# The last token block's tail moved behind the first feed-forward units, and the second product moved into the first one's buffers

## The chip, the core and the metric

The kernel runs on one core of a Trainium2 chip. The metric is device microseconds of one execution. Five engines work side by side: PE (TensorE, the matrix products), DVE (VectorE), ACT (ScalarE), POOL (GpSimd) and SP (SyncE, which here issues every DMA). Each engine runs its own instructions strictly in order; they meet through semaphores.

## What is computed

One transformer block of 2048 tokens by 1024 features, all in fp32. Cut to what matters here:

```python
y = concat([o, y_lru]) @ w_out                       # attention and recurrence, then the out product
x = layer_norm(ALPHA * x + g1 * y, ln1_g, ln1_b)
h = modulate(layer_norm(x), sh2, sc2)
a, b = split(h @ w_ffn_in, 2)                        # first product, 1024 x 5632
f = (silu(a) * b) @ w_ffn_out                        # second product, 2816 x 1024
out = layer_norm(ALPHA * x + g2 * f, ln2_g, ln2_b)
```

## The kernel before, in words

Every fp32 operand of PE is kept as two rounded tiles, a high part (a cast on ACT) and the remainder (a subtraction on DVE or POOL); `mm3` (lines 140 to 144) makes one product out of three matrix instructions, L142, L143 and L144. Everything around the change is written in Python order; a scheduler moves instructions within an engine where priorities and buffers let it, and buffers come from rings ("pools") whose size sets how far ahead a producer may run.

**Out product, L1037 to L1076.** Sixteen token tiles (`out_tile`), four to a token block. The residual `x` of a tile is loaded just ahead of it into a ring of SBUF tiles.

**Tail of a token block, L1078 to L1118.** When four tiles are done, a generator `after` gives the block's tail in 21 steps: `norm1` (L1083: layer norm, times `lg` at L1086, plus `lb` at L1089, both 128x1024 on POOL), `norm2` (a second layer norm), and `lift2` (L1101: eight steps, each four PE transposes at L1105, an ACT evacuation L1107 and a store into `h2_d`). The tail of block b is stepped inside the out tiles of block b+1. Block 3 has no block behind it, so its tail is drained by `while tails: step()` before the feed-forward's code begins.

**First product.** The two halves of the tokens (`tb`) are taken one after the other; each is multiplied by 22 column groups, 44 units in all. A unit (`Unit`, L1170 to L1248) is a 2x2 block product with seven sub-products (Strassen and Winograd's form), each of 12 matrix instructions, 84 to a unit. `prep` loads and combines weights on POOL (L1189 to L1194), casts them (L1198, ACT) and subtracts (L1199, DVE); a ring of 9 weight tiles `w` lets it run ahead. `build(tb, k)` (L1145 to L1169) makes the token operands of one quarter k of the contraction: reload from `h2_d`, combine, and split into the `B` and `T` tiles. Units 0 and 1 begin the first half: four products that need only the operands `B11` and `B21`, made ahead by `lift2`, with the four builds between them. `sliced` runs a unit quarter by quarter, and unit 21 is sliced with the builds of the second half behind its quarters. The last instruction of a unit on DVE is L1246, and its results go to `hid_d` in DRAM.

**Second product, L1290 to L1379.** All first-product buffers are closed, and new ones opened. 32 tiles (16 token tiles by two column halves) of 22 contraction steps, 66 matrix instructions each. `prep_w2` (L1307) loads a weight tile into one of 4 raw buffers, casts it (L1311) and subtracts (L1312); 25 `w2` tiles are held. `load_hid` (L1317) loads a token tile's hidden values as two pieces of 704 KB, one tile ahead. The output chain of a tile begins with L1359; the last one's is the end of the kernel.

These lines set the order around the change:

```python
        while tails:              # L1128: block 3's tail, drained here
            step()
...
    ahead(4)
    for k, (u, p) in enumerate(((units[0], 1), (units[0], 2), (units[1], 1), (units[1], 2))):
        build(0, k)
        whole(u, (p,))
```

Of the kernel before, what the change touches and what calls it, by code (L numbers as in the profile page):

```python
# [60 lines left out]
def kernel(ctx: ExitStack, tc: tile.TileContext, x, cx, prm_d, wa1, wa2, b_ada, w_in, w_v, lqk,  # L61
# [924 lines left out]
    s5 = ExitStack()  # L986
    fe = s5.enter_context(tc.tile_pool(name="fe", bufs=1, reuse_waits="tile"))
    toks = {(n, k): fe.tile([P, 2, 512], F32R, tag=f"{n}{k}", name=f"{n}_{k}") for n in ("B11", "B21") for k in range(4)}
    rawp = s5.enter_context(tc.tile_pool(name="rawp", bufs=3, reuse_waits="tile"))
    sp_ = s5.enter_context(tc.tile_pool(name="sp5", bufs=1, reuse_waits="tile"))  # L990
    qp = s5.enter_context(tc.tile_pool(name="qp5", bufs=6, reuse_waits="tile"))

    with ExitStack() as s4:
        wps = {k: s4.enter_context(tc.tile_pool(name=f"wo{k}", bufs=1, side="right", reuse_waits="tile"))
               for k in (4, 5, 6, 7, 0, 1, 2, 3)}
        oyp = s4.enter_context(tc.tile_pool(name="oyp", bufs=2, side="right", reuse_waits="tile"))
        psW = s4.enter_context(tc.tile_pool(name="psW", bufs=2, space=PSUM, side="right", reuse_waits="tile"))
        psL = s4.enter_context(tc.tile_pool(name="psL", bufs=1, space=PSUM, reuse_waits="tile"))
        psX = s4.enter_context(tc.tile_pool(name="psX", bufs=2, space=PSUM, reuse_waits="tile"))

        xq = s4.enter_context(tc.tile_pool(name="xq", bufs=7, side="right", reuse_waits="tile"))
# [4 lines left out]
        lnq = s4.enter_context(tc.tile_pool(name="ln4", bufs=1, side="right", reuse_waits="tile"))  # L1006
        lg = lnq.tile([P, D], F32, tag="lg", name="lg")
        lb = lnq.tile([P, D], F32, tag="lb", name="lb")
        tp = s4.enter_context(tc.tile_pool(name="tp", bufs=2, side="right", reuse_waits="tile"))
        xtile = lambda n: (tp.tile([P, D], F32, tag="x", name="x4", bufs=4) if 1 <= n % 11 <= 4 else  # L1010
                           xq.tile([P, D], F32, tag="xq", name="xq"))
# [18 lines left out]
        tails = []  # L1030

        def step():
            for t in list(tails):
                if next(t, 0) == 0:
                    tails.remove(t)

        def out_tile(b, i, rh, xs, mv):  # L1037
            ti = 4 * b + i
            oy = oyp.tile([P, 2, 8, P], F32R, tag="oy", name="oy")
            dma(oy.rearrange("p a k t -> p (a k) t"),  # L1040
                oy_d[b].rearrange("p a k t -> p (a k) t")[:, :, i * P:(i + 1) * P])
            xt = xtile(ti)
            dma(xt, x[ti * P:(ti + 1) * P, :])
            xv = xt.rearrange("p (a b) -> p a b", a=2)

            def mms(ps, kk, st, en):
                lh, ll = oy[:, 0, kk], oy[:, 1, kk]
# [24 lines left out]
            with tc.high_priority(offset=100):  # L1072
                V.tensor_tensor(xv, pl, xv, ALU.add)
            ln_stats(xt, mv, i)
            xs.append(xt)

        def affine(xs, mv, rs):
            nb = sm.tile([P, 4], F32, tag="nb", name="nb")  # L1078
            V.scalar_tensor_tensor(nb, mv[:, 0], -1.0, rs, ALU.mult, ALU.mult)
            for i, xt in enumerate(xs):  # L1080
                S.activation(xt, xt, AF.Identity, bias=nb[:, i:i + 1], scale=rs[:, i:i + 1])

        def norm1(xs, mv):  # L1083
            affine(xs, mv, rsqrt(mv[:, 1], 4, LN_EPS))
            for i, xt in enumerate(xs):
                G.tensor_tensor(xt, xt, lg, ALU.mult)  # L1086
            yield
            for i, xt in enumerate(xs):
                G.tensor_tensor(xt, xt, lb, ALU.add)  # L1089
                yield  # L1090

        def norm2(b, xs):
            mw = sm.tile([P, 2, 4], F32, tag="mv", name="mw", bufs=4)
            for i, xt in enumerate(xs):
                dma(x1_d[4 * b + i], xt)
                ln_stats(xt, mw, i)
                yield
            affine(xs, mw, rsqrt(mw[:, 1], 4, LN_EPS))
            yield

        def lift2(b, xs):  # L1101
            for k in range(KD):
                ps = psX.tile([P, 512], F32, tag="x", name="ps_x")
                for i in range(4):
                    PE.transpose(ps[:, i * P:(i + 1) * P], xs[i][:, k * P:(k + 1) * P], ident)  # L1105
                hf = tp.tile([P, 512], F32, tag="hf", name="hf4", bufs=2)
                S.activation(hf, ps, AF.Identity, bias=mod2[:, k:k + 1], scale=mod2[:, 8 + k:9 + k])  # L1107
                dma(h2_d[b][:, k], hf)
                if b == 0:
                    t = toks["B11" if k < 4 else "B21", k % 4]  # L1110
                    S.copy(t[:, 0], hf)
                    G.tensor_tensor(t[:, 1], hf, t[:, 0].bitcast(F32), ALU.subtract)
                yield

        def after(b, xs, mv):
            yield from norm1(xs, mv)
            yield from norm2(b, xs)
            yield from lift2(b, xs)  # L1118

        for b in range(NB):  # L1120
            rh = head_norm(b)
            xs = []
            mv = sm.tile([P, 2, 4], F32, tag="mv", name="mv4", bufs=4)
            for i in range(4):
                out_tile(b, i, rh, xs, mv)
            tails.append(after(b, xs, mv))
            step()
        while tails:  # L1128
            step()

    opp = [s5.enter_context(tc.tile_pool(name=f"opp{k}", bufs=1, side="right", reuse_waits="tile")) for k in range(4)]
# [128 lines left out]
    def whole(u, ps):  # L1263
        for p in ps:
            u.mms(p, range(4), True, True)
            ahead(1)
# [17 lines left out]
    for u in units[2:NJ - 1]:  # L1284
        whole(u, std)
# [154 lines left out]
```

## Time and profile before

| | |
|---|---|
| median of 3 runs | 2962.98 us (2962.23 to 2969.71) |
| the profiled execution | 2965.58 us, its span 2963.8 us, mean granted clock 0.97 |
| busy: PE, DVE, POOL, ACT | 94%, 66%, 48%, 47% of the span |
| chain that ended last | PE 67%, DVE 7%, ACT 3%, DMA 3% |
| stages, us from the start | attention to about 1360, out product to 1540, first product to 2448, second to 2952, output of the last tile to 2963.8 |

The span is the time on the core from the first instruction to the last; the execution's own time is 1.8 us more. With PE at 94% a stage is read by what PE waited for in it, in the list of waits, and by whether it did its instructions at the full clock.

### The profile page before, as it was taken

What the parts mean: (1) busy time and instruction counts of PE and PEld (TensorE: products, weight loads), DVE (VectorE), ACT (ScalarE), POOL (GpSimd) and SP (SyncE); (2) the same over time, 40 slices, a digit from 0 to 9 for tenths busy, and PEclk for the clock granted to TensorE, in tenths of its full rate; (3) what the DMA queues carried; (4) which work ended last, traced back from release to release, by engine and by line L of the source; (5) the groups of instructions that cost most, each with busy time, mean ns of one, the idle gap of its engine ahead of it and who ended that gap; (6) DMA issues with size and microseconds to landing.
All of it is one profiled execution on the core that took longest, in us unless ns stands there. A gap on an engine that the chain in (4) does not pass through costs nothing.

```text
span 2963.8 us, 37341 instructions
## 1 busy us (share of the span) xinstructions
PE 2776.1 (94%) x13452; PEld 2316.7 (78%) x13452; DVE 1955.0 (66%) x3202; ACT 1407.1 (47%) x1907; POOL 1421.9 (48%) x891
## 2 busy tenths in 40 slices
PE   8989889878999999999985999999999998999998
PEld 4868767766899999887864888887888886887886
DVE  7755796487899989986886655558655545225554
ACT  3537568744777777763344333334333324113332
POOL 2014643455788888861535444445444433222443
PEclk9999999989999999999997999999999999999999
DMA  8874636366132312135563222223222218434542
GB/s 332 313 217 167 215 116 256 113 219 184 36 85 64 81 58 70 54 140 195 193 200 114 93 86 82 84 84 104 93 82 82 84 52 291 146 129 162 172 165 93
DMA packets 223193, 407.94 MB, mean 138 GB/s; under 512 B 20888, under 2 KB 110104, under 8 KB 220448
## 3 DMA queue, kind: packets, MB, share of 16 engines
q1 hardware_dynamic: 223008, 405.55, 41.2%
q8 instruction: 106, 1.74, 0.2%
q14 instruction: 79, 0.65, 0.1%
HBM read 281.74 MB, written 123.75 MB: 137 GB/s over the span
## 4 chain that ended last, share of the span: by engine, by line
PE 67%; DVE 7%; ACT 3%; DMA 3%; issue 1%; POOL 1%; SPq 0%; ACTq 0%; DVEq 0%; POOLq 0%
PE ps L143 9%; PE ps L144 9%; PE ps L142 9%; PE ps_s L846 8%; PE ps_f L142 5%; PE ps_f L143 5%; PE ps_f L144 5%; PE pt L927 4%; PE po L921 2%; PE po L922 2%; PE po L920 2%; DMA w2r<-in_w 1%; DVE e L848 1%; PE ps_w L1050 1%; PE ps_l L1050 1%
## 5 line engine op out<-in xcount | busy, mean ns | idle before, releaser
L848 DVE TENSOR_SCALAR_CACHE_REDUCE e<-ps_s 128x768 f32<-128x768 f32 x384 | 359.6, 951 | 37.7 <-PE ps_s L846 29.6
L864 POOL TENSOR_TENSOR a<-e,e 128x768 f32<-128x768 f32 x192 | 349.2, 1848 | 17.2 <-PE pt L927 12.5
L846 PE MATMUL ps_s<-k,q 128*128 128x384 f32 x1536 | 336.7, 351 | 15.1 <-DVE e L848 13.7
L853 ACT ACTIVATE e<-e,nm 128x2304 f32<-128x2304 f32 x128 | 285.3, 2229 | 51.8 <-DVE nm L852 48.7
L846 PEld LDWEIGHTS ps_s<-k,q 128*128 128x128 f32 x1536 | 267.9, 191 | 31.0 <-DVE e L848 23.9
L1324 POOL TENSOR_TENSOR hid<-hf,hid 128x1408 fp32r<-128x1408 f32 x32 | 104.8, 3276 | 293.9 <-ACT hid L1323 293.9
L931 ACT CAST ah<-pt 128x512 fp32r<-128x512 f32 x288 | 165.8, 582 | 127.7 <-PE pt L927 125.4
L932 DVE TENSOR_TENSOR al<-pt,ah 128x512 fp32r<-128x512 f32 x288 | 195.7, 685 | 33.7 <-ACT ah L931 33.4
L1323 ACT CAST hid<-hf 128x1408 fp32r<-128x1408 f32 x64 | 87.8, 1375 | 248.0 <-PE ps_f L144 232.0
L861 POOL TENSOR_SCALAR e<-e,rr,rn 128x2304 f32<-128x2304 f32 x64 | 146.4, 2287 | 92.5 <-DVE nm L852 49.6
L142 PE MATMUL ps_p<-ht,w 128*128 128x512 f32 (+1 forms) x416 | 162.8, 392 | 16.0 <-DVE kf L204 10.8
L927 PEld LDWEIGHTS pt<-ident,a 128*128 128x128 f32 x1152 | 144.5, 141 | 42.0 <-POOL a L864 3.3
L927 PE MATMUL pt<-ident,a 128*128 128x128 f32 x1152 | 174.7, 274 | 2.6 <-POOL a L864 2.4
L1189 POOL TENSOR_TENSOR s<-w1r 128x512 f32<-128x512 f32 x44 | 58.0, 1317 | 233.5 <-DMA w1r<-in_w 228.2
L144 PE MATMUL ps_p<-ht,w 128*128 128x512 f32 (+1 forms) x416 | 161.8, 390 | 8.2 <-DVE w L174 8.2
L143 PE MATMUL ps_p<-ht,w 128*128 128x512 f32 (+1 forms) x416 | 161.5, 388 | 0.0
L210 POOL TENSOR_TENSOR lo<-kf,hi 128x512 fp32r<-128x512 f32 (+1 forms) x36 | 58.7, 1632 | 176.5 <-ACT hi L209 140.8
L1194 POOL TENSOR_TENSOR s<-w1r,s 128x512 f32<-128x512 f32 x44 | 73.1, 1661 | 126.9 <-DVE w__15147 L1199 5.6
L920 PE MATMUL po<-ah,v 128*128 128x512 f32 x288 | 126.3, 438 | 0.6 <-ACT ah L931 0.6
L921 PE MATMUL po<-al,v 128*128 128x512 f32 x288 | 116.9, 406 | 3.1 <-DVE al L932 1.4
L922 PE MATMUL po<-ah,v 128*128 128x512 f32 x288 | 114.5, 398 | 0.0
L1324 DVE TENSOR_TENSOR hid<-hf,hid 128x1408 fp32r<-128x1408 f32 x32 | 54.4, 1701 | 86.2 <-ACT hid L1323 86.2
(3085 smaller groups left out, 8258.8 us busy)
## 6 DMA issues: line engine op xcount, KB each, us to landing
w1r<-in_w SPq DMA_DIRECT2D x88, 512.0 KB, 3.5
hf<-hid_d SPq DMA_DIRECT2D x64, 704.0 KB, 4.2
hid_d<-hid SPq DMA_DIRECT2D x88, 256.0 KB, 2.2
wraw<-in_w_in SPq DMA_DIRECT2D x32, 512.0 KB, 5.1
adaw<-in_wa SPq DMA_DIRECT2D x32, 512.0 KB, 4.7
q<-q_d SPq DMA_DIRECT2D x64, 256.0 KB, 4.9
oy<-oy_d SPq DMA_DIRECT2D x16, 1024.0 KB, 6.2
x<-in_x SPq DMA_DIRECT2D x24, 512.0 KB, 8.9
```

The source lines that it names most:

```text
L142: PE.matmul(ps, lhsT=lh, rhs=rh, start=start, stop=False)
L143: PE.matmul(ps, lhsT=lh, rhs=rl, start=False, stop=False)
L144: last["pe"] = PE.matmul(ps, lhsT=ll, rhs=rh, start=False, stop=stop).ins
L846: PE.matmul(ps[:, j, :384], lhsT=q[:, m, part, qt * P:(qt + 1) * P], rhs=kst[h, m][:, c0:c0 + 384], start=(part == 0), stop=(part == 1))
L848: V.tensor_scalar(et[:, cc * 768:(cc + 1) * 768].rearrange("p (a b) -> p a b", a=2), ps[:, :, :384], -0.125, None, ALU.mult, ALU.min, accu ...
L853: S.activation(et, et, AF.Exp, bias=nm[:, m:m + 1], scale=-1.0, accum_out=ss[m])
L864: last["a"] = G.tensor_tensor(a, es[0][:, g * 768:(g + 1) * 768], es[1][:, g * 768:(g + 1) * 768], ALU.add).ins
L920: PE.matmul(po, lhsT=vh, rhs=ah, start=(j == 0), stop=False)
L921: PE.matmul(po, lhsT=vh, rhs=al, start=False, stop=False)
L922: PE.matmul(po, lhsT=vl, rhs=ah, start=False, stop=(j == NKT - 1))
L927: PE.transpose(pt[:, qt * P:(qt + 1) * P], ath[h, b, qt, j // 6][:, (j % 6) * P:(j % 6 + 1) * P], ident)
L932: V.tensor_tensor(al, pt, ah.bitcast(F32), ALU.subtract)
```

## The change

**The tail of block 3 is no longer drained.** It is put on the list `tails` after the out product and stepped (`late`) behind each product of unit 1's last five and of units 2 to 5, held behind the last instructions that those products issued on ACT, DVE and POOL. `norm1` gives its four `lg` products one to a step for this block.

**The first product is prepared earlier.** Its helpers and left-hand pools are made before the out product; the first three weight tiles are prepared after out tile (3,1), and the first build's loads are issued after (3,2). The residual tiles of the out product lie in other pools, some of them shared with the first product's weights; on SP the load of out tile 1's residual now follows those of `lg`, `lb`, three later residuals and one weight. The ring of weight tiles has 5 tiles while the tail lives, then 11, and 7 near the end. Of PSUM banks the products use 6 while the tail lives, then 8.

**The second product takes the first one's slots.** Its pools are gone; w2 tiles lie in the slots of the token operands, and the last unit is sliced so that each quarter, when done, frees slots, and issues loads of hidden values and five w2 tiles (`begin`). A token tile's hidden values come in three loads (512, 512 and 384 KB) and six casts. Token tiles 0 and 1 are multiplied together, so a w2 tile serves two products.

```diff
@@ norm1
-        def norm1(xs, mv):
+        def norm1(xs, mv, dealt):
             affine(xs, mv, rsqrt(mv[:, 1], 4, LN_EPS))
             for i, xt in enumerate(xs):
+                if dealt and i:
+                    yield
                 G.tensor_tensor(xt, xt, lg, ALU.mult)
@@ the out product's loop and the first product
                 out_tile(b, i, rh, xs, mv)
-            tails.append(after(b, xs, mv))
-            step()
+                if (b, i) == (3, 1):
+                    ahead(3)
+                if (b, i) == (3, 2):
+                    qs0 = load_q4(0, 0)
+            if b < NB - 1:
+                tails.append(after(b, xs, mv))
+                step()
         while tails:
             step()
+        tails.append(after(NB - 1, xs, mv))
...
+    def late():
+        with tc.issue_after(last["A5"]), tc.issue_after(last["V5"]), tc.issue_after(last["G5"]):
+            step()
...
+    def new_w():
+        n = 5 if tails else 11 if turn5["n"] < 14 * NJ - 14 else 7
...
-    ahead(4)
+    ahead(1)
     for k, (u, p) in enumerate(((units[0], 1), (units[0], 2), (units[1], 1), (units[1], 2))):
-        build(0, k)
+        build(0, k, None if k else qs0)
         whole(u, (p,))
-    ahead(3)
+    ahead(1)
     sliced(units[0], rest, range(4))
-    whole(units[1], rest)
-    for u in units[2:NJ - 1]:
+    whole(units[1], rest, late)
+    for u in units[2:6]:
+        whole(u, std, late)
+    ahead(2)
+    for u in units[6:NJ - 1]:
         whole(u, std)
@@ the second product
-    sliced(units[-1], std, range(3, -1, -1))
-    s5.close()
-    ps5.close()
+    def load_hid(n, q):
+        i = n % 16
+        w = min(8, NJ - q * 8)
+        raw = x4p.tile([P, 8, P], F32, tag="x", name="hf6")[:, :w]
+        dma(raw, hid_d[i // 4][i % 4, :, q * 8:q * 8 + w, :])
+        for r in range(2):
...
+            S.copy(t[:, 0], raw[:, 4 * r:4 * r + w])
+            (G if m in (1, 4) else V).tensor_tensor(t[:, 1], raw[:, 4 * r:4 * r + w], t[:, 0].bitcast(F32),
+                                                    ALU.subtract)
+    def begin(k):
+        if k < 3:
+            load_hid(0, k)
+        else:
+            load_hid(1, 0)
+        for j in range(5 * k, 5 * k + 5):
+            prep_w2(0, j)
+    sliced(units[-1], std, range(4), begin)
...
+        if n != 1:
+            pss = {m: new_bank() for m in ((0, 1) if n == 0 else (n,))}
+            for j in range(NJ):
+                for m, ps in pss.items():
+                    h, w = hts[m, j // 4], w2t[hf, j]
+                    mm3(ps, h[:, 0, j % 4], h[:, 1, j % 4], w[:, 0], w[:, 1], j == 0, j == NJ - 1)
```

Three places show how instructions stand. On PE at the end of the out product, before (`ps_l` is the last out tile's bank, `ps_x` a transposed tile, `w__15084` the first product's first weight tile):

```order
L1051 MATMUL ps_l<-wo_13335,oy 128x512
L1054 MATMUL ps_l<-wo_13335,oy 128x512 x2
L1105 MATMUL ps_x<-ident,xq 128x128 x24
L142 MATMUL ps<-B_0_13273,w__15084 128x512
L143 MATMUL ps<-B_0_13273,w__15084 128x512
```

and with the change (L1282 is the transpose, `w__14706` the first weight tile):

```order
L1229 MATMUL ps_l<-wo_13347,oy 128x512 x2
L1282 MATMUL ps_x<-ident,x_14129 128x128
L1282 MATMUL ps_x<-ident,x_14200 128x128
L1282 MATMUL ps_x<-ident,x_14288 128x128
L1282 MATMUL ps_x<-ident,x_14395 128x128
L1282 MATMUL ps_x<-ident,x_14129 128x128
L1282 MATMUL ps_x<-ident,x_14200 128x128
L1282 MATMUL ps_x<-ident,x_14288 128x128
L1282 MATMUL ps_x<-ident,x_14395 128x128
L142 MATMUL ps<-B_0_13276,w__14706 128x512
L143 MATMUL ps<-B_0_13276,w__14706 128x512
L144 MATMUL ps<-B_0_13276,w__14706 128x512
```

Of block 2's 24 transposes eight now stand ahead of the first product, eight inside its second sub-product and eight behind its third; block 3's 32 begin some 330 rows further on.

On POOL the eight `lg` and `lb` operations of block 3, before, among the builds (L1161, L1166):

```order
L1166 TENSOR_TENSOR qT<-qT,qB_15156 128x512
L1086 TENSOR_TENSOR x_14539<-x_14539,lg 128x1024
L1161 TENSOR_TENSOR qB_15199<-qB_15201,qB_15199 128x512
L1086 TENSOR_TENSOR x_14610<-x_14610,lg 128x1024
L1086 TENSOR_TENSOR x_14698<-x_14698,lg 128x1024
L1089 TENSOR_TENSOR x_14539<-x_14539,lb 128x1024
L1086 TENSOR_TENSOR x_14805<-x_14805,lg 128x1024
L1089 TENSOR_TENSOR x_14610<-x_14610,lb 128x1024
L1089 TENSOR_TENSOR x_14698<-x_14698,lb 128x1024
L1166 TENSOR_TENSOR qT<-qT,qB_15203 128x512
L1089 TENSOR_TENSOR x_14805<-x_14805,lb 128x1024
```

and with the change, where L1263 and L1266 are the two operations, L1053 to L1058 weights, L1097 and L1098 a unit's sums:

```order
L1056 TENSOR_TENSOR s_15330<-w1r 128x512
L1098 TENSOR_TENSOR q<-u,q 128x512
L1263 TENSOR_TENSOR x_14545<-x_14545,lg 128x1024
L1263 TENSOR_TENSOR x_14616<-x_14616,lg 128x1024
L1263 TENSOR_TENSOR x_14721<-x_14721,lg 128x1024
L1266 TENSOR_TENSOR x_14545<-x_14545,lb 128x1024
L1263 TENSOR_TENSOR x_14836<-x_14836,lg 128x1024
L1053 TENSOR_TENSOR s_15480<-w1r 128x512
L1266 TENSOR_TENSOR x_14616<-x_14616,lb 128x1024
L1266 TENSOR_TENSOR x_14721<-x_14721,lb 128x1024
L1266 TENSOR_TENSOR x_14836<-x_14836,lb 128x1024
L1054 TENSOR_TENSOR s_15481<-s_15480,w1r 128x512
```

The eight still stand nearly together, now between the POOL work of units 2 and 3, with one weight operation among them.

On SP at the end of the first product, before (`hf` a hidden piece, `w2r` a raw w2 tile, `hid_d` a unit's store):

```order
L70 DMA hid_d_90<-hid 128x4x128
L70 DMA hf_21663<-hid_d_88 128x1408
L70 DMA hf_21668<-hid_d_88 128x1408
L70 DMA hf_21783<-hid_d_88 128x1408
L70 DMA g2b<-mod_d 128x1024
L70 DMA w2r<-in_w 128x512 x4
```

and with the change:

```order
L70 DMA hf_21540<-hid_d_88 128x1024
L70 DMA hf_21594<-hid_d_88 128x1024
L70 DMA hid_d_91<-hid 128x4x128
L70 DMA hf_21648<-hid_d_88 128x768
L70 DMA hid_d_90<-hid 128x4x128
L70 DMA hf_21723<-hid_d_88 128x1024
L70 DMA w1r<-in_w 128x1024
L70 DMA hid_d_91<-hid 128x4x128
L70 DMA hid_d_90<-hid 128x4x128
L70 DMA w2r<-in_w 128x512 x2
```

The first hidden pieces now stand ahead of the last unit's weights, and the first w2 tiles ahead of its last stores.

## Rows read from the trace of the kernel before

**Rows 1.** Waits of PE, 1440 to 2964 us: waiter, releaser, us, times, longest.
```profile
PE ps L142 <- ACT w__15084 L1198: 33.0, 1, 33.0
PE ps_x L1105 <- ACT hf L1107: 10.0, 7, 3.0
PE ps_f L142 <- ACT w__21675 L1311: 8.7, 1, 8.7
...
PE ps_f L142 <- ACT w__23152 L1311: 1.7, 1, 1.7
```

**Rows 2.** Timeline of DVE (start, us, instruction): ends of units 4, 20, 26 and 43.
```profile
1698.36 0.68 DVE L1246 TENSOR_TENSOR hid<-g,u 128x512 f32<-128x512 f32 x1
...
2003.00 0.68 DVE L1246 TENSOR_TENSOR hid<-g,u 128x512 f32<-128x512 f32 x1
...
2126.37 0.68 DVE L1246 TENSOR_TENSOR hid<-g,u 128x512 f32<-128x512 f32 x1
...
2452.17 0.68 DVE L1246 TENSOR_TENSOR hid<-g,u 128x512 f32<-128x512 f32 x1
```

**Rows 3.** Timeline of PE: last out tile, transposes, unit 20's and the first product's end.
```profile
1539.92 0.62 PE L1054 MATMUL ps_l<-wo,oy 128*128 128x512 f32 x2
1540.38 1.03 PE L1105 MATMUL ps_x<-ident,xq 128*128 128x128 f32 x8
...
2001.26 0.39 PE L144 MATMUL ps<-T,w__18080 128*128 128x512 f32 x1
...
2448.31 0.39 PE L144 MATMUL ps<-T,w__21505 128*128 128x512 f32 x1
```

**Rows 4.** Timeline of DVE, second product: output chains of tiles 2, 14, 17 and 31.
```profile
2511.22 0.69 DVE L1359 TENSOR_TENSOR f<-ps_f,g2b 128x512 f32<-128x512 f32 x1 [1.61 <-PE ps_f L144]
...
2690.74 0.69 DVE L1359 TENSOR_TENSOR f<-ps_f,g2b 128x512 f32<-128x512 f32 x1 [4.45 <-PE ps_f L144]
...
2743.23 0.69 DVE L1359 TENSOR_TENSOR f<-ps_f,g2b 128x512 f32<-128x512 f32 x1 [1.46 <-PE ps_f L144]
...
2952.66 0.69 DVE L1359 TENSOR_TENSOR f<-ps_f,g2b 128x512 f32<-128x512 f32 x1 [5.61 <-PE ps_f L144]
```

**Rows 5.** Timelines of POOL, DVE and ACT in PE's 33 us of idle time.
```profile
1558.09 5.08 POOL L1086 TENSOR_TENSOR x<-x,lg 128x1024 f32<-128x1024 f32 x2
...
1568.63 5.53 POOL L1089 TENSOR_TENSOR x<-x,lb 128x1024 f32<-128x1024 f32 x2
...
1560.90 5.57 DVE L1156 TENSOR_TENSOR T<-qT,T 128x512 fp32r<-128x512 f32 x2
...
1574.64 0.68 DVE L1156 TENSOR_TENSOR B<-qB,B 128x512 fp32r<-128x512 f32 x1
...
1571.99 0.62 ACT L1155 CAST T<-qT 128x512 fp32r<-128x512 f32 x1 [12.06 <-DVE qT L1163]
...
1580.44 0.61 ACT L1198 CAST w__15084<-w1r 128x512 fp32r<-128x512 f32 x1
```

**Rows 6.** Windows: us, then busy us and count of PE, PEld, DVE, ACT, POOL; clock, DMA share, GB/s.
```profile
1600.00:1610.00 10.00, 5.22 (x21) 4.03 (x22) 2.38 (x4) 4.78 (x8) 5.21 (x4) 0.50 0.58 192
...
1620.00:2020.00 400.00, 400.00 (x1766) 331.23 (x1765) 219.58 (x307) 142.75 (x240) 181.29 (x126) 1.00 0.27 87
...
2460.00:2470.00 10.00, 7.61 (x25) 5.41 (x25) 2.18 (x5) 2.86 (x4) 3.17 (x1) 0.82 1.05 411
...
2500.00:2700.00 200.00, 200.00 (x884) 165.62 (x883) 61.05 (x66) 41.16 (x34) 46.03 (x14) 1.00 0.45 148
```

**Rows 7.** Timelines of SP and ACT at the second product's start.
```profile
2444.65 2.85 SPq L70 DMA_DIRECT2D hf<-hid_d  x3
...
2453.74 2.00 SPq L70 DMA_DIRECT2D hid_d<-hid  x2
...
2459.81 2.52 SPq L70 DMA_DIRECT2D w2r<-in_w  x4
...
2456.75 0.62 ACT L1311 CAST w__21675<-w2r 128x512 fp32r<-128x512 f32 x1 [1.68 <-DMA w2r<-in_w]
```

**Rows 8.** Timeline of ACT: the residual of out tile 1 lands.
```profile
1360.24 1.06 ACT L1068 ACTIVATE x<-x 128x1024 f32<-128x1024 f32 x1 [2.75 <-DMA x<-in_x]
```

More of the change, by code (lines that the diff above doesn't have):

```diff
@@ L986 @@
     s5 = ExitStack()
[L987 to L991, printed above, removed]
+    ps5 = ExitStack()
+    pool5 = lambda n, bufs, **kw: s5.enter_context(tc.tile_pool(name=n, bufs=bufs, reuse_waits="tile", **kw))
@@ new lines, with load_q4 @@
+    x4p = pool5("x4", 4)
+    fe = pool5("fe", 1)
+    toks = {(n, k): fe.tile([P, 2, 512], F32R, tag=f"{n}{k}", name=f"{n}_{k}") for k in range(4) for n in ("B11", "B21")}
+    rawp = pool5("rawp", 3)
+    sp_ = pool5("sp5", 1)
+    lnq = pool5("ln4", 1)
+    xqa = pool5("xqa", 3)
+    qp = pool5("qp5", 6)
+    psX = ps5.enter_context(tc.tile_pool(name="psX", bufs=2, space=PSUM, reuse_waits="tile"))
+    opp, wopB = [], []
+    def load_q4(tb, k):
+        q = {}
+        for n, (s, kk) in (("B11", (0, k)), ("B12", (1, k)), ("B22", (1, k + 4)), ("B21", (0, k + 4))):
+            q[n] = qp.tile([P, 512], F32, tag="q", name="q" + n)
+            dma(q[n], h2_d[2 * tb + s][:, kk])
+        return q
@@ new lines, in build, with split @@
+    def build(tb, k, q=None):
+        q = q or load_q4(tb, k)
+        t1 = qp.tile([P, 512], F32, tag="q", name="qT")
+        def split(n, src):
+            if tb == 0 and n in ("B11", "B21"):
+                return
+            t = (fe if n in ("B11", "B21") else opp[k]).tile([P, 2, 512], F32R, tag=f"{n}{k}", name=f"{n}_{k}")
+            S.copy(t[:, 0], src)
+            V.tensor_tensor(t[:, 1], src, t[:, 0].bitcast(F32), ALU.subtract)
+            toks[n, k] = t
+        split("B11", q["B11"])
+        V.tensor_tensor(t1, q["B12"], q["B11"], ALU.subtract)
+        G.tensor_tensor(q["B12"], q["B22"], q["B12"], ALU.subtract)
+        split("T1", t1)
+        V.tensor_tensor(t1, q["B22"], t1, ALU.subtract)
+        split("T2", t1)
+        split("B21", q["B21"])
+        G.tensor_tensor(t1, t1, q["B21"], ALU.subtract)
+        split("T3", q["B12"])
+        split("B22", q["B22"])
+        split("T4", t1)
@@ new lines, with new_bank @@
+    turn5 = {"w": 0, "p": 0, "n": 0}
+    def new_w():
+        n = 5 if tails else 11 if turn5["n"] < 14 * NJ - 14 else 7
+        i = turn5["w"] % n
+        turn5["w"] = i + 1
+        turn5["n"] += 1
+        pool, tag = ((xqa, "xq") if i < 3 else (wopB[0], "w") if i < 5 else (lnq, "lg" if i == 5 else "lb") if i < 7
+                     else (x4p, "x"))
+        return pool.tile([P, 2, 4, P], F32R, tag=tag, name="w1_")
+    def new_bank():
+        n = 6 if tails else 8
+        i = turn5["p"] % n
+        turn5["p"] = i + 1
+        pool, tag = (psR, "p") if i < 4 else (psQ, "p") if i < 6 else (psX, "x")
+        return pool.tile([P, 512], F32, tag=tag, name="ps")
@@ new lines, with step @@
+    tails = [None]
+    def step():
+        for t in list(tails):
+            if t and next(t, 0) == 0:
+                tails.remove(t)
+    def late():
+        with tc.issue_after(last["A5"]), tc.issue_after(last["V5"]), tc.issue_after(last["G5"]):
+            step()
+    std = (1, 6, 5, 2, 7, 3, 4)
+    rest = (6, 5, 7, 3, 4)
+    units = [Unit(tb, j) for tb in range(2) for j in range(NJ)]
+    preps = [(units[0], 1), (units[0], 2), (units[1], 1), (units[1], 2)]
+    preps += [(u, p) for u in units[:2] for p in rest] + [(u, p) for u in units[2:] for p in std]
@@ new lines, with ahead, whole, sliced @@
+    preps = iter(preps)
+    def ahead(n):
+        for _ in range(n):
+            u, p = next(preps, (None, 0))
+            if u:
+                u.prep(p)
+    def whole(u, ps, each=lambda: None):
+        for p in ps:
+            u.mms(p, range(4), True, True)
+            ahead(1)
+            each()
+    def sliced(u, ps, ks, after=lambda k: None):
+        for n, k in enumerate(ks):
+            for p in ps:
+                u.mms(p, [k], n == 0, n == 3)
+                if n == 3:
+                    ahead(1)
+            after(k)
@@ L1028, in head_norm @@
             return rh
[L1030 to L1035, printed above, removed]
+        tails.clear()
         def out_tile(b, i, rh, xs, mv):
@@ L1249 @@
-    banks = [0]
-    std = (1, 6, 5, 2, 7, 3, 4)
-    rest = (6, 5, 7, 3, 4)
-    units = [Unit(tb, j) for tb in range(2) for j in range(NJ)]
-    preps = [(units[0], 1), (units[0], 2), (units[1], 1), (units[1], 2)]
-    preps += [(u, p) for u in units[:2] for p in rest] + [(u, p) for u in units[2:] for p in std]
-    preps = iter(preps)
-    def ahead(n):
-        for _ in range(n):
-            u, p = next(preps, (None, 0))
-            if u:
-                u.prep(p)
[L1263 to L1266, printed above, removed]
@@ L1268, in sliced @@
-    def sliced(u, ps, ks, after=lambda k: None):
-        for n, k in enumerate(ks):
-            for p in ps:
-                u.mms(p, [k], n == 0, n == 3)
-                if n == 3:
-                    ahead(1)
-            after(k)
-    ahead(4)
+        tails.append(after(NB - 1, xs, mv))
+    opp.extend(pool5(f"opp{k}", 1, side="right") for k in range(4))
+    wopB.append(pool5("wopB", 2, side="right"))
+    ua = pool5("ua5", 2)
+    s5b = ExitStack()
+    ub = s5b.enter_context(tc.tile_pool(name="ub5", bufs=1, reuse_waits="tile"))
@@ L1289, with prep_w2 @@
         whole(u, std)
-    sliced(units[-1], std, range(3, -1, -1))
+    w2t, hts = {}, {}
+    w2slots = [(opp[k], f"{n}{k}") for k in range(4) for n in ("T2", "T1", "T3", "B22", "T4")]
+    w2slots += [(wopB[0], "w")] * 2 + [(xqa, "xq")] * 3
+    hslots = [(fe, f"{n}{k}") for k in range(4) for n in ("B11", "B21")] + [(rawp, "w1r")] * 3 + [(lnq, "lg")]
+    def prep_w2(hf, j):
+        n = hf * NJ + j
+        raw = ua.tile([P, 512], F32, tag="ug"[n % 2], name="w2r")
+        dma(raw, w2[j * P:(j + 1) * P, hf * 512:(hf + 1) * 512])
+        pool, tag = w2slots[n % 25]
+        w = w2t[hf, j] = pool.tile([P, 2, 512], F32R, tag=tag, name="w2_")
+        S.copy(w[:, 0], raw)
+        V.tensor_tensor(w[:, 1], raw, w[:, 0].bitcast(F32), ALU.subtract)
@@ new lines, in begin @@
+    def begin(k):
+        if k < 3:
+            load_hid(0, k)
+        else:
+            load_hid(1, 0)
+        for j in range(5 * k, 5 * k + 5):
+            prep_w2(0, j)
+    sliced(units[-1], std, range(4), begin)
+    s5b.close()
+    lnp = s5.enter_context(tc.tile_pool(name="ln6", bufs=1, reuse_waits="tile"))
+    for j in range(20, NJ):
+        prep_w2(0, j)
+    for q in (1, 2):
+        load_hid(1, q)
+    g2b = lnp.tile([P, D], F32, tag="g2b", name="g2b")
+    stt = lnp.tile([P, 16, 2, 6], F32, tag="stt", name="stt")
```

320 lines of the change are left out of this document (133 added, 187 removed).

## The prediction

> **What bounds the kernel now.** I read the page for the busy shares first: PE works 94% of the span, so the question is only where the other time lies. The list of PE's waits over the last two stages [rows 1] answers it: one wait of 33.0 us before the very first weight tile of the first product, 10.0 us in small waits of the transposes, 8.7 us at the start of the second product, and small ones at its middle. Between these places PE is full: the windows [rows 6] show 1766 matrix instructions in 400 us and 884 in 200 us at clock 1.00, 0.2265 us each. Waits alone understate a stall, because the clock falls after one: in 1600 to 1610 PE did 21 instructions in 10 us at a granted clock of 0.50, the lower of its two levels, 1.2 GHz, after having idled in the transposes before.
>
> So I count each stall by distance instead, against what PE does undisturbed. Units 4 to 20 end 2003.00 - 1698.36 = 304.64 us apart, 19.04 us a unit [rows 2]; tiles 2 to 14 end 179.52 us apart, 14.96 us a tile [rows 4]. Both make 0.2267 us an instruction. A unit's last instruction on DVE starts 1.74 us after its last product starts (2003.00 and 2001.26, [rows 2, 3]).
>
> - Start of the first product. The next instruction after the last out tile could go at 1540.15, unit 4 was done at about 1698.36 - 1.51 = 1696.85. Five units are 95.2 us, and 56 transposes at 1.03 us for eight are 7.2 us; call it 8 with their slower part. Lost: 156.7 - 95.2 - 8 = 53.5 us.
> - Second half's builds. Units 20 to 26 took 123.37 us for 114.24: lost 9.1 us.
> - Start of the second product. The last product of the first ended at about 2448.54 [rows 3]; to tile 2's chain at 2511.22 [rows 4] are 62.5 us, for three tiles' 44.9: lost 17.6 us.
> - Its second weight half. Tiles 15 to 17 took 2743.23 - 2690.74 = 52.5 us for 44.9: lost 7.6 us. Tiles 18 to 31 lose nothing (209.43 us for 14).
>
> **Why the first wait is so long.** The weight needs nothing but a cast. But ACT stands for 12.06 us ahead of it in the cast of a build, waiting for a DVE subtraction, and reaches the weight only at 1580.44 [rows 5]. DVE is late because its subtractions take 2.8 us each (5.57 for two) where one takes 0.68 us elsewhere; and they do so just while POOL runs the tail's 128x1024 operations, at 2.54 and 2.77 us each. So the drained tail costs in two ways: its own length, and through DVE.
>
> **The change part by part.**
>
> *Start of the first product.* The tail's POOL block no longer stands among the first builds, the first three weights are cast before the out product ends, and the first build's loads are there. The 33.0 us wait and the transposes' 10 us go: the transposes stand among products that fill the gaps. What is late next is the builds. The four have 7 two-operand DVE instructions each, 28 in all, and some 12 weight subtractions and evacuations stand between them: 40 x 0.69 = 28 us without disturbance. PE has 48 instructions that need no build, and 60 of unit 0's rest, 24.5 us, and 24 transposes, 3.6 us: 28 us. Bounds: no loss, or, with the builds' own eight POOL operations stretching DVE as above for some 13 us, 13 x (1 - 0.69/2.8) = 10 us. The nearest row is the second half's builds, where 36 such instructions cost 9.1 us; 28 make 7. I take 7.
>
> *The tail beside units 1 to 5.* Its PE and ACT work costs what is counted above. Its POOL block is 4 x 2.54 + 4 x 2.77 = 21.2 us, nearly in one piece between the POOL work of units 2 and 3; POOL is busy 181.29 of 400 us and DVE 219.58 in undisturbed units [rows 6]. In 21.2 us DVE has 7.8 products' work to do and, at 2.8 us for a subtraction and about as much again for the rest, gets through some five, so it falls some 7 us behind. The weights in the ring of five are 13.6 us of work for PE. Bounds: the ring covers it, 0, or nothing covers it, and the weights' sums wait behind the block on POOL too, 11. I take 4, nearer the cover.
>
> A rule of the Trainium skill speaks against this placement: its GPSIMD Engine Reference, section Specifications, says that GpSimd shares its SBUF interfaces with VectorE, in contention with DVE instructions that have two SBUF inputs. The trace agrees: 2.8 us beside POOL, 0.68 without [rows 5]. By the rule alone, every subtraction in the block would wait, and the sum would stand at the upper bound, 7 us more than I take.
>
> *Out product.* The residual of tile 1 landed just in time, ACT having waited 2.75 us for it [rows 8]. It now stands behind six more loads on SP. At the 411 GB/s of [rows 6] 512 KB take 1.3 us, so it comes up to 8 us later, and PE has work of the attention's end beside it: 0 to 5, I take 3.
>
> *Second half's builds.* Unchanged but for a ring of 11 weights instead of 9: 9.1 stays.
>
> *Start of the second product.* Before, SP issued three hidden loads at 2444.65 ahead of any w2 load, the first w2 cast came at 2456.75, and the next four w2 loads went only at 2459.81, behind two stores [rows 7]; the DMA engines were full in 2460 to 2470, 411 GB/s [rows 6]. Now the first hidden pieces and w2 loads stand ahead of the last unit's stores, weights are cast while that unit runs, and a w2 tile serves two products, so 22 tiles are wanted over 29.9 us instead of 15. The 17.6 us should go to 0 to 8; I take 2.
>
> *Second weight half.* Nothing about its four raw buffers changes: 7.6 stays. Six smaller pieces a tile instead of two cost ACT under 1 us a tile beside 14.96 us of products: covered by the double buffering that also stands before. I allow 3 us for the stage.
>
> *Sum.* First product: 53.5 - 7 - 4 - 3 = 39.5 us gained. Second: 17.6 - 2 - 3 = 12.6. Together 52.1. The profiled execution's 2965.58 becomes 2913.5; it stands 2.6 us above the median shown, so I expect **2911 us**.
>
> **The rivals.**
>
> *The tail's block costs as much beside the products as before them.* For it: DVE's 2.8 us, the rule above, and that PE falls to half clock after a stall [rows 6]. Against: DVE is half idle in these units, and five weights are ahead. Its place is units 2 to 4; it gives the upper bounds, 10 + 11 + 5 us, and some 8 more of half clock: 20 us more than the forecast, 2931.
>
> *The start of the second product stays stalled.* For: the same four raw buffers, the same DMA volume at 411 GB/s, and the last unit's quarters now issue loads while its stores wait. Against: the new order on SP. It takes back 17.6 - 2 = 16 us: 2927.
>
> *Nothing is late.* The ring covers the tail, the builds end in time and the second product starts smoothly: 2911 - 7 - 4 - 3 - 5 = 2892.
>
> *Slower.* The hidden pieces become a wait in every tile of the second product: three loads pass through four slots, and a slot is held until two casts and two subtractions, one of them on POOL, are done. Thirty tiles give back the gain at 52.1 / 30 = 1.7 us a tile, and more than 2.0 us a tile is slower by over 0.3%. For: SP carries half as many loads again. Against: before, the tiles had the same depth of two, and 884 instructions in 200 us show no wait. The time then is 2972 us and up.
>
> **How the numbers follow.** Forecast, 2898 to 2924: 0.53. Tail's block: 0.19. Second start: 0.13. Nothing late: 0.10. Slower: 0.05. The range reaches from a little below "nothing late", 2888, to the two middle rivals partly together (2911 + 20 + 10): 2942; about 0.1 lies above and below. The runs of this kernel tell 0.3%, 8.9 us, from no change; a time within that of 2963 needs both middle rivals and more. So faster 0.92, same 0.03, slower 0.05.
>
> **What would show it.** Right: no wait of 33 us at the first product's first weight; unit 4's end about 39 us earlier; DVE's subtractions at over 2 us only beside the tail's POOL block; PE's waits in units 0 to 5 of 10 to 15 us in all, on `T` tiles and weights; tile 2 of the second product some 55 us earlier; tile 16's dip still there. Wrong: a wait of over 15 us on a weight in units 2 to 5, a first w2 wait of over 5 us, or tiles of the second product that end more than 14.96 us apart in its steady part.

## The result

The changed kernel takes 2916.34 us (median of 4 runs, 2915.73 to 2919.35) against 2962.61 us for the kernel before in the same comparison: a ratio of 0.984, 95% interval 0.982 to 0.986. It is faster by 46 us, and lies 5 us above the 2911 us forecast. Its profiled execution has a span of 2913.9 us, 49.9 us less.

The time is made up by stages from five marks on the trace: the last value product of attention on PE, the end of the last out tile, the end of unit 10, the output chain of tile 2 of the second product, and that of tile 31. Units after the tenth, and tiles between the marks, take the same time in both kernels except where the text says so.

| us between marks | before | changed | difference | forecast |
|---|---|---|---|---|
| out product | 181.2 | 189.2 | +8.0 | +3 |
| transposes and units 0 to 10 | 272.1 | 241.9 | -30.2 | -42.5 |
| unit 10 to tile 2 of the second product | 698.6 | 679.0 | -19.6 | -15.6 |
| tile 2 to tile 31 | 441.4 | 433.8 | -7.6 | +3 |

So the sum came out nearly right because its errors cancel: by these marks the first half of the change gained 17 us less than forecast, the second half 15 us more. The mark at unit 10 is DVE's last instruction there, and it stands 1.74 us behind the start of the unit's last matrix instruction before, and 3.41 us in the changed kernel and in all its variants below (unit 20 shows the same: 1977.00 and 1980.41 us in the timelines below, 2001.26 and 2003.00 in [rows 2, 3]). By PE's own work 1.7 us of the third row's gain therefore belong to the second: -31.9 and -17.9 us, so that the first half gained 16 us less and the second 13 us more. That they cancel is luck.

The page of the changed kernel gives PE 95% of its span. The list of PE's waits, from the out product to the end, answers to [rows 1] (waiter, releaser, us in all, times, longest):

```profile
PE ps_w L1225 <- DVE x L1245: 10.4, 5, 3.8
PE ps L144 <- DVE w__15535 L1063: 3.4, 1, 3.4
PE ps L142 <- ACT w__14984 L1062: 2.7, 1, 2.7
PE ps_x L1282 <- ACT hf L1287: 2.6, 1, 2.6
...
PE ps L142 <- ACT T L1019: 2.2, 2, 1.6
...
PE ps L144 <- DVE w__15398 L1063: 1.2, 1, 1.2
```

The 33.0 us are gone, and no wait of the second product is left at all. Instead the out product has 10.4 us (before: 5.3 us in the same lines), and the first units have small waits on weights. The timelines of DVE and PE answer to [rows 2], [rows 3] and [rows 4]: the ends of units 4, 20 (on both engines) and 26, and the chains of tiles 2, 14, 17 and 31.

```profile
1675.77 0.68 DVE L1108 TENSOR_TENSOR hid<-g,u 128x512 f32<-128x512 f32 x1
...
1977.00 0.39 PE L144 MATMUL ps<-T,w__18084 128*128 128x512 f32 x1
1980.41 0.68 DVE L1108 TENSOR_TENSOR hid<-g,u 128x512 f32<-128x512 f32 x1
...
2103.39 0.68 DVE L1108 TENSOR_TENSOR hid<-g,u 128x512 f32<-128x512 f32 x1
...
2468.97 0.69 DVE L1431 TENSOR_TENSOR f<-ps,g2b 128x512 f32<-128x512 f32 x1 [2.73 <-PE ps L144]
...
2648.49 0.69 DVE L1431 TENSOR_TENSOR f<-ps,g2b 128x512 f32<-128x512 f32 x1 [2.73 <-PE ps L144]
...
2693.37 0.69 DVE L1431 TENSOR_TENSOR f<-ps,g2b 128x512 f32<-128x512 f32 x1 [2.13 <-PE ps L144]
...
2902.81 0.69 DVE L1431 TENSOR_TENSOR f<-ps,g2b 128x512 f32<-128x512 f32 x1 [5.60 <-PE ps L144]
```

Unit 4 ends 22.6 us earlier than before, where the prediction named about 39, and tile 2's chain 42.2 us earlier, where it named 55. Units 20 to 26 take 122.98 us, so the second half's builds cost 8.7 us, as before (9.1). Tiles 14 to 17 take 44.88 us, three times 14.96: the dip at the second weight half, 7.6 us before, is gone too, which the prediction did not expect.

**Where the out product lost.** DVE's and PE's timelines at the second out tile of block 3:

```profile
1515.25 1.70 DVE L1063 TENSOR_TENSOR w__14706<-w1r,w__14706 128x512 fp32r<-128x512 f32 x1
...
1518.07 1.70 DVE L1063 TENSOR_TENSOR w__14709<-w1r,w__14709 128x512 fp32r<-128x512 f32 x1
...
1519.81 1.63 DVE L1063 TENSOR_TENSOR w__14716<-w1r,w__14716 128x512 fp32r<-128x512 f32 x1
...
1523.88 0.80 PE L1225 MATMUL ps_w<-wo,oy 128*128 128x512 f32 x1 [3.84 <-DVE x L1245]
```

The three weights that the change prepares early have their subtractions here, each 1.6 to 1.7 us instead of 0.68, since POOL is at block 2's last `lb` operations and, beside the third, at an operation of a build. The out tiles' own DVE work (L1245), which frees PE's banks, stands behind them. The windows show what that does, in the first line; the second is the place in the tail's block, and the third the start of the second product:

```profile
1520.00:1530.00 10.00, 6.16 (x17) 4.79 (x17) 10.00 (x15) 1.09 (x2) 0.90 (x1) 0.66 0.78 280
...
1620.00:1630.00 10.00, 6.42 (x24) 4.49 (x23) 9.17 (x15) 2.29 (x4) 10.00 (x6) 0.92 0.50 195
...
2430.00:2440.00 10.00, 10.00 (x46) 8.27 (x45) 7.28 (x9) 3.43 (x7) 3.55 (x3) 1.00 0.74 235
```

In 1520 to 1530 us PE did 17 matrix instructions where 44 fit: a wait of 3.84 us costs 6, the rest through a mean granted clock of 0.66.

**The tail's block** on POOL, and DVE beside it:

```profile
1606.45 7.97 POOL L1263 TENSOR_TENSOR x<-x,lg 128x1024 f32<-128x1024 f32 x3 [3.83 <-ACT x L1256]
...
1612.10 2.87 DVE L1063 TENSOR_TENSOR w__15418<-s,w__15418 128x512 fp32r<-128x512 f32 x1
1614.89 0.68 DVE L1091 TENSOR_TENSOR v<-ps,u 128x512 f32<-128x512 f32 x1
...
1617.20 2.84 POOL L1263 TENSOR_TENSOR x<-x,lg 128x1024 f32<-128x1024 f32 x1
...
1617.71 2.88 DVE L1063 TENSOR_TENSOR w__15460<-w1r,w__15460 128x512 fp32r<-128x512 f32 x1
```

The subtractions take 2.9 us again, as before in [rows 5]; an instruction with one operand in PSUM, between them, takes its 0.68. The last two lines show the size of such a hold: POOL's instruction ends at 1620.04 us and DVE's at 1620.59. It is so throughout the traces of the kernel before and of the changed one: of the 128x512 DVE `TENSOR_TENSOR` instructions behind 1540 us whose two operands both lie in SBUF, 331 begin while a POOL instruction runs, and 330 of these end 0.54 to 0.64 us after that instruction does (the other one began within 0.01 us of it); the 802 others take 0.70 us at most.

### The profile page after: what moved, and what is told of

The parts are those of the page before. It is cut to its first block, busy times and chain, and to the rows that moved or that the text cites. A ratio compares the mean times of both kernels' runs of the same rounds, so it can differ in the third digit from the quotient of the medians.

```text
span 2913.9 us, 37631 instructions
## 1 busy us (share of the span) xinstructions
PE 2765.6 (95%) x13452; PEld 2310.3 (79%) x13452; DVE 2013.6 (69%) x3298; ACT 1433.6 (49%) x2039; POOL 1409.1 (48%) x923
## 3 DMA queue, kind: packets, MB, share of 16 engines
q8 instruction: 106, 1.74, 0.3%
## 4 chain that ended last, share of the span: by engine, by line
PE 66%; DVE 7%; ACT 3%; issue 2%; POOL 2%; DMA 2%; SPq 0%; DVEq 0%; ACTq 0%; POOLq 0%
PE ps L143 14%; PE ps L144 14%; PE ps L142 14%; PE ps_s L846 8%; PE pt L927 4%; PE po L921 2%; PE po L922 2%; PE po L920 2%; DVE e L848 1%; PE ps_w L1225 1%; PE ps_w L1226 1%; PE ps_w L1229 1%; PE ps_l L1225 1%; PE ps_l L1229 1%; PE ps_l L1226 1%
## 5 line engine op out<-in xcount | busy, mean ns | idle before, releaser
L1376 ACT CAST hid<-hf 128x512 fp32r<-128x512 f32 x192 | 111.5, 586 | 281.2 <-PE ps L144 266.5
L1377 POOL TENSOR_TENSOR hid<-hf,hid 128x512 fp32r<-128x512 f32 x64 | 83.6, 1306 | 315.9 <-ACT hid L1376 315.9
L1377 DVE TENSOR_TENSOR hid<-hf,hid 128x512 fp32r<-128x512 f32 (+1 forms) x128 | 95.8, 751 | 157.1 <-ACT hid L1376 157.0
L861 POOL TENSOR_SCALAR e<-e,rr,rn 128x2304 f32<-128x2304 f32 x64 | 146.4, 2288 | 90.3 <-DVE nm L852 49.9
L1053 POOL TENSOR_TENSOR s<-w1r 128x512 f32<-128x512 f32 x44 | 59.3, 1348 | 270.3 <-DMA w1r<-in_w 254.2
L1097 POOL TENSOR_TENSOR v<-v,q 128x512 f32<-128x512 f32 x44 | 72.1, 1639 | 145.1 <-DVE u L1096 145.1
```

Of the source, the lines that this page charges most:

```text
L1377: (G if m in (1, 4) else V).tensor_tensor(t[:, 1], raw[:, 4 * r:4 * r + w], t[:, 0].bitcast(F32), ALU.subtract)
```

## The experiments

All are read by the same five marks. The runs that share a stage's code tell how far it scatters: the changed kernel twice, and the two edits of the second product, give 189.2, 190.7, 189.8 and 189.7 us for the out product and 241.9, 241.9, 240.5 and 240.4 us for units 0 to 10. Each kernel has one trace, so a mark is one execution's.

| kernel | median us | out product | units 0 to 10 | to tile 2 | tiles 2 to 31 |
|---|---|---|---|---|---|
| changed, again | 2914.89 | 190.7 | 241.9 | 679.1 | 434.3 |
| weights' subtractions later | 2912.13 | 185.2 | 240.5 | 677.8 | 433.8 |
| tail drained | 2943.20 | 186.8 | 268.6 | 679.1 | 434.0 |
| tiles 0 and 1 apart | 2919.30 | 189.8 | 240.5 | 683.5 | 433.8 |
| loads late | 2923.65 | 189.7 | 240.4 | 687.6 | 431.9 |
| tail spread | 2913.13 | 190.8 | 238.9 | 679.0 | 434.7 |
| tail on DVE | 2913.56 | 189.3 | 236.5 | 679.0 | 433.9 |
| later, spread | 2909.66 | 185.2 | 239.0 | 678.5 | 433.8 |
| later, on DVE | 2905.62 | 185.0 | 235.8 | 677.6 | 433.8 |
| later, spread, on DVE | 2905.91 | 183.6 | 233.4 | 678.6 | 433.8 |

**The changed kernel again**, on the chip of the last edits.

> The changed kernel itself, on the chip of this batch, so that the small edits are compared on one chip: 0.984 of the kernel before, 2915 to 2920 us. If the ratio is 0.982 instead, the edits measured so far gained less than their ratios say.

2914.89 us (2912.80 to 2920.55), 0.983 of the kernel before (0.981 to 0.984): between the two values named. Differences of 2 us between medians are therefore not read below; the marks are.

**The tail's place.**

```diff
+    while tails:
+        step()
     ahead(1)
     for k, (u, p) in enumerate(((units[0], 1), (units[0], 2), (units[1], 1), (units[1], 2))):
```

> The changed kernel with block 3's tail drained before the feed-forward again; early weights, first loads and the new second product are kept. Theory A, the tail's place is what the first product gained: PE waits 20 to 30 us before or in the first units again, unit 20 ends 20 to 25 us later than 1980 us, the time is 2936 to 2943 us. Theory B, the early weights and loads are what gained, since the 33 us wait was the first weight's cast in ACT's queue: at most 10 us are lost, 2916 to 2926 us.

2943.20 us, 0.993 of before (0.991 to 0.994), 28 us over the changed kernel, and nearly all of it in units 0 to 10: 268.6 us, against 272.1 before and 241 with the tail moved. PE's waits there:

```profile
PE ps_x L1282 <- ACT x L1256: 18.2, 4, 16.9
PE ps L142 <- ACT T L1019: 8.7, 2, 7.9
```

Theory A holds, at the upper edge of its times. With the tail drained, PE stands for its transposes, which come behind the eight POOL operations, and then for the builds. With no tail left on the list this kernel also has the ring of 11 weight tiles and 8 banks from the first unit on; what these do there was not tried apart. The early weights and loads by themselves are worth some 5 us there (272.1 - 268.6, and 1.7 for the later mark), and the out product of that kernel takes 5.6 us more than before, so that in that kernel they gain nothing in sum.

**The weights' subtractions.**

```diff
-                if (b, i) == (3, 1):
-                    ahead(3)
                 if (b, i) == (3, 2):
                     qs0 = load_q4(0, 0)
+                    with tc.issue_after(last["vo"]):
+                        ahead(3)
```

Here `last["vo"]` is the DVE instruction that ends the third out tile of block 3.

> The changed kernel with the first three weight tiles' subtractions held on DVE until block 3's third out tile is done (about 1537 us) instead of among the second one's work (1515 to 1521 us, 1.70, 1.70 and 1.63 us each beside POOL's lg and lb operations of block 2). Theory A, these subtractions held up the out product: PE's wait of 3.8 us at 1524 us goes, the last out tile ends 5 to 6 us earlier than 1548 us, the time falls to 2909 to 2912 us. Theory B, the out product is late because residuals are loaded later on SP: the wait stays and the time is 2915 to 2918 us.

The out product falls from 189.2 to 185.2 us, and the subtractions take 0.68 us each at their new place:

```profile
1537.07 0.68 DVE L1063 TENSOR_TENSOR w__14824<-w1r,w__14824 128x512 fp32r<-128x512 f32 x1
```

```profile
1520.00:1530.00 10.00, 10.00 (x45) 8.00 (x44) 10.00 (x16) 2.36 (x4) 5.41 (x3) 1.00 0.97 351
```

The window of the loss above has 45 instructions at full clock. Theory A holds; the time, 2912.13 us (ratio 0.982, 0.980 to 0.983), is just at the upper end of what it gave. The 4 us understate the edit. Behind the wait for tile 1's residual, this run's granted clock fell, as in the second run of the changed kernel and not in its first; the window 1370 to 1380 us in the changed kernel, in its second run and in this one:

```profile
1370.00:1380.00 10.00, 9.81 (x43) 8.11 (x44) 7.79 (x9) 4.18 (x4) 1.80 (x2) 1.00 0.99 358
...
1370.00:1380.00 10.00, 8.19 (x29) 6.32 (x28) 5.14 (x4) 3.89 (x4) 0.00 (x0) 0.83 1.03 383
...
1370.00:1380.00 10.00, 8.08 (x29) 6.16 (x28) 3.85 (x3) 3.18 (x3) 0.00 (x0) 0.83 1.07 394
```

Against the second run, with 190.7 us, the edit gives back 5.5 us, which is what theory A said. Some 4 us of the out product's loss remain (185.2 against 181.2); they arise in its first 20 us, around that wait, and nothing here was tried on them.

**Sharing w2 tiles, and loading early.** In the first of two kernels, tiles 0 and 1 are multiplied one after the other; in the second they stay together, but all loads of the last unit's quarters come after its last quarter.

```diff
-        if n != 1:
-            pss = {m: new_bank() for m in ((0, 1) if n == 0 else (n,))}
+        if True:
+            pss = {n: new_bank()}
```

> The changed kernel with token tiles 0 and 1 of the second product multiplied one after the other, each w2 tile wanted every 0.68 us at first. Theory A, sharing the w2 tiles is what freed the start of its stall: PE waits 6 to 12 us on w2 tiles and the time is 2922 to 2928 us. Theory B, loading and casting them while the last unit runs is enough: no wait over 2 us, 2915 to 2919 us.

```diff
-    sliced(units[-1], std, range(4), begin)
+    sliced(units[-1], std, range(4))
+    for k in range(4):
+        begin(k)
```

> The changed kernel with all hidden-value loads and w2 preparations of the last unit issued after its last quarter instead of after each; tiles 0 and 1 still together. Theory A, issuing them early is what freed the second product's start: PE waits 8 to 15 us there and the time is 2924 to 2934 us. Theory B, two tiles together need half the w2 rate and that is enough: a first wait of 3 to 5 us and 2918 to 2922 us.

Apart, the stage takes 4.5 us more than 679.0; with late loads 8.6 us more, of which 1.9 come back behind tile 2. Neither run fits a theory as it was written. Apart, 2919.30 us lies at theory B's upper edge, and the waits, 2.0 us at most, are theory B's, but the stage is not free. With late loads, 2923.65 us lies between the two theories, and the waits are under what either named. Their longest waits:

```profile
PE ps L143 <- DVE w__21733 L1363: 2.0, 1, 2.0
```

```profile
PE ps L142 <- ACT w__21634 L1362: 1.9, 1, 1.9
```

The waits are small against what the stage lost; the rest is short idle times and a lower clock, as the window of the second kernel shows, where 45 instructions fit and 28 were done:

```profile
2420.00:2430.00 10.00, 7.56 (x28) 5.53 (x28) 6.15 (x10) 5.03 (x9) 3.79 (x3) 0.88 0.78 244
```

So each part without the other leaves some of the start's loss: of the 17.8 us lost before, counted from the start of the first product's last instruction to tile 2's chain, 0.2 are lost with both, 4.7 without the sharing and 8.4 with the loads late. A kernel without both was not run, nor were the smaller hidden pieces alone, so what those pieces brought is open.

**The dip at the second weight half**, tried on the kernel before, since the change does not aim at it:

```diff
-                (G if q else V).tensor_tensor(t[:, 1], raw, t[:, 0].bitcast(F32), ALU.subtract)
+                V.tensor_tensor(t[:, 1], raw, t[:, 0].bitcast(F32), ALU.subtract)
```

The theory comes from these lines of the kernel before, on POOL, DVE and SP:

```profile
2709.81 3.23 POOL L1324 TENSOR_TENSOR hid<-hf,hid 128x1408 fp32r<-128x1408 f32 x1 [14.34 <-ACT hid L1323]
...
2709.82 3.77 DVE L1360 SCALAR_TENSOR_TENSOR y<-y,f 128x512 f32<-128x512 f32 x1
...
2713.62 0.33 SPq L70 DMA_DIRECT2D y_d<-y  x1
2714.94 0.33 SPq L70 DMA_DIRECT2D w2r<-in_w  x1
```

A POOL instruction of 3.23 us holds a DVE instruction that takes 0.69 us elsewhere; the store of its result waits at the head of SP's queue, and the w2 loads stand behind the store.

> The kernel before with one edit: both pieces of a token tile's hidden values are subtracted on DVE, none on POOL (POOL's 128x1408 subtraction took 3.28 us). Theory A, the dip at the second weight half (7.6 us lost over tiles 15 to 17) came from that POOL instruction: beside it a DVE two-input operation of tile 14's output took 3.77 us, the store of y waited for it at the head of SP's queue, and four w2 loads behind the store went late. Then tiles 15 to 17 take 45 to 47 us instead of 52.5, and the time is 5 to 8 us under the kernel before. Theory B, four raw w2 buffers and the DMA engines set the dip: it stays at 6 to 9 us and the time is within 3 us of before.

2960.56 us, 0.998 of before (0.997 to 0.999), some 5 us less. The chains of tiles 14 and 17 in that kernel:

```profile
2690.65 0.69 DVE L1359 TENSOR_TENSOR f<-ps_f,g2b 128x512 f32<-128x512 f32 x1 [4.45 <-PE ps_f L144]
...
2735.53 0.69 DVE L1359 TENSOR_TENSOR f<-ps_f,g2b 128x512 f32<-128x512 f32 x1 [1.07 <-PE ps_f L144]
```

44.88 us: no loss at all, with the same four raw buffers. So POOL's subtraction is the cause; the way from it over the store in SP's queue is read from the lines above and was not tried apart; one more such hold, of 3.22 us on a weight's subtraction at 2692.80 us, went with the same edit. In the changed kernel POOL's pieces are 512 wide and take 1.31 us, so that such a hold is short. That this is why the changed kernel has no dip fits, but no run of the changed kernel shows it.

**The tail's block on POOL.** Two edits: spread it, or give it to DVE.

```diff
-            each()
+            if m % every == 0:
+                each()
...
-    whole(units[1], rest, late)
-    for u in units[2:6]:
-        whole(u, std, late)
+    whole(units[1], rest, late, 2)
+    for u in units[2:8]:
+        whole(u, std, late, 2)
```

> The changed kernel with block 3's tail stepped behind every second product of units 1 to 7 instead of every product of units 1 to 5, so that POOL's eight operations stand as five and three with five weight operations between. Theory A, the block in one piece is what made PE wait (DVE's subtractions at 2.3 to 2.9 us from 1607 to 1630 us, waits of 3.4, 1.2 and 1.1 us on weights): units 2 to 6 end 4 to 8 us earlier, the time is 0.15 to 0.3% lower than the changed kernel's. Theory B, the same sum of POOL time beside DVE costs the same however it is dealt: within 2 us.

```diff
-                G.tensor_tensor(xt, xt, lg, ALU.mult)
+                (V if dealt else G).tensor_tensor(xt, xt, lg, ALU.mult)
...
-                G.tensor_tensor(xt, xt, lb, ALU.add)
+                (V if dealt else G).tensor_tensor(xt, xt, lb, ALU.add)
```

> The changed kernel with block 3's eight lg and lb operations on DVE instead of POOL, 8 x 1.3 = 10.4 us more for DVE and 21 us less for POOL. Theory A, sharing between DVE and POOL is what cost: no subtraction there takes over 2 us except beside weights' sums, PE's waits in units 2 to 5 fall from some 10 us to 3 to 6, the time is 3 to 6 us under the changed kernel's. Theory B, DVE is short of time there whatever stretches it: 10.4 us more work make the waits as long or longer, and the time is 0 to 6 us over the changed kernel's.

Spread, units 0 to 10 take 238.9 us, some 2 us less: nearer theory B, and small against the scatter of 1.5 us. On DVE they take 236.5, some 4.7 us less, although DVE does 8 x 1.22 us more work, and no weight's subtraction beside it takes over 1.4 us:

```profile
1616.98 1.22 DVE L1263 TENSOR_TENSOR x<-x,lg 128x1024 f32<-128x1024 f32 x1
...
1619.86 0.69 DVE L1063 TENSOR_TENSOR w__15418<-s,w__15418 128x512 fp32r<-128x512 f32 x1
```

PE's waits in units 2 to 5 fall from 8.6 to 4.6 us in all, as theory A of the second edit said (2.6 us of that fall is the wait of a transpose for ACT, which is gone); the median fell by less than its 3 us, with the marks showing 4.7. So on POOL the block costs more than the same work costs on the busier DVE. Two things go with it, the hold between DVE and POOL and the wait of POOL's weight sums behind the block; how much each cost was not measured apart.

**Together.**

> Both edits together: weights' subtractions held behind the third out tile and the tail stepped behind every second product. If both theories A hold and the two add up, 0.3 to 0.5% under the changed kernel, 2902 to 2908 us against a before of 2963; if spreading does nothing, as the first edit alone, 2909 to 2912 us.

> Weights' subtractions held behind the third out tile, and the tail's eight operations on DVE. If both effects add up (5 and 4 us), 8 to 10 us under the changed kernel of this batch; PE waits 4 to 6 us less over units 0 to 10 than with the first edit alone. If DVE's extra 10.4 us only move the wait, 4 to 6 us under it.

> The same with the tail stepped behind every second product as well. The wait of 3.2 us on a weight that stood behind the run of lg operations on DVE should go: 9 to 13 us under the changed kernel, PE's waits in units 2 to 8 under 4 us. If the scheduler bunches the operations anyway, no difference to the kernel without spreading.

2909.66, 2905.62 and 2905.91 us. The first is what the later subtractions alone were to give, so spreading adds nothing in the time. The later subtractions and the tail on DVE add up, 9 us under the changed kernel of the same batch, ratio 0.980 of before (0.978 to 0.981). Spreading on top shortens units 0 to 10 by 2.4 us more by the marks, and PE's longest waits on weights to

```profile
PE ps L142 <- ACT w__14984 L1062: 1.9, 1, 1.9
PE ps L144 <- DVE w__15500 L1063: 1.6, 1, 1.6
```

but the median does not show it, and PE's waits on weights in units 2 to 8 are 4.4 us, not under 4. The version to keep is the one with the later subtractions and the tail's eight operations on DVE.

## Why the prediction was right, and where its steps were off

- **The tail's place** was the main gain, as said: drained again, it costs 28 us. Of the two ways that the prediction named, the run shows the tail's own length on PE's path: 16.9 us for `x`, which comes through the eight POOL operations, and 7.9 us for a build behind them. The other way, DVE held beside POOL, is seen in the traces but was not priced apart. The rule cited from the Trainium skill (GPSIMD Engine Reference, section Specifications: SBUF interfaces shared with VectorE for instructions with two SBUF inputs) is one that the trace agrees with: 2.87 us for a subtraction beside the block, 0.68 us for an instruction that reads PSUM.
- **Builds, 7 us.** PE's idle time and clock from 1550 to 1590 us make 7.9 us. Close.
- **The tail beside units 1 to 5, 4 us.** By the same reckoning 1600 to 1640 lost 7.8 us, inside the bounds of 0 and 11 but on the side that the rule spoke for; the ring of five weights covered less than was taken. And 1650 to 1670 lost 4.4 us, 2.6 of it a transpose waiting for ACT: the step "its PE and ACT work costs what is counted above" was wrong there. The three stretches make 20.1 us; by PE's work the stage still loses 21.6, where the prediction left 11.
- **Out product, 3 us.** It lost 8.0. The residual of tile 1, which the prediction priced, cost some 1.6 us in the profiled execution (PE 17.3 us busy in 1360 to 1380 where it was 18.9), and 1.5 more where the clock fell behind it. The larger part was not priced at all: the change puts three weights' subtractions on DVE in the middle of the out tiles. The prediction said that these weights are cast before the out product ends and counted that at nothing; the cover it would have had to name, DVE's free time, was short: DVE was busy 33.3 of 40 us from 1500 to 1540 us in the kernel before already. Moved, they gave back 4 to 5.5 us.
- **Start of the second product.** The loss before, by its own marks, is 17.8 us and not 17.6. 2 us were to remain, 0.2 did. Two parts do it together, as the two runs show.
- **Second weight half: "nothing about its four raw buffers changes: 7.6 stays".** Wrong, and here the mechanism failed and not only a size. The buffers did not set the dip; POOL's long subtraction did, by the trace through a held DVE instruction and a store at the head of SP's queue. The change made POOL's pieces shorter.
- **Six pieces a tile, 3 us.** They cost nothing: tiles 2 to 14 end 179.52 us apart, as before.

The rival on the other side, a wait in every tile of the second product, did not come. The first rival, the tail's block costing as much beside the products, was priced at 20 us over the forecast, 2931 us; the first half of the change came out 16 us over, the tail's part of it over that rival's bound of 11 (7.8 and 4.4 us), and without the 13 us that the second half gave beyond the forecast the time would have been about 2929. So the forecast was right in what it moved and why that pays, and that its 2911 us was nearly met is luck. The total error of 5 us hides errors of 16 and 13; the rest is that the profiled execution stood 2.6 us above the median before and 0.6 below it with the change.

## What to carry to other kernels

Work taken off an engine's critical stage is paid for where it is put: ask of each moved instruction which engine it lands on there, what stands behind it in order, and what runs beside it on POOL. In these traces a POOL instruction costs a DVE instruction with two SBUF operands that begins beside it the rest of its own length, so short POOL pieces, or the work on DVE itself, can be cheaper although DVE is the busier engine. Measure a stall by the distance between marks against the undisturbed rate; the list of waits shows only part of it (3.84 us of 6 in the out product).

## What was not expected of the hardware

A POOL instruction of 3.23 us made one DVE instruction of 0.69 us last 3.77 us, and without it a loss of 7.6 us went; by the trace it went through the order of one DMA queue. That the eight operations cost less on DVE, which spent 9.8 us on them, than on POOL was also not expected by the prediction, which never considered moving them there.
